# Two halves of a PSUM tile cast first, both remainders after: the key tiles of two head pairs in an attention layer on one Trainium2 core

## The chip, the cores and the metric

The kernel runs on one core of a Trainium2 chip. The metric is the device time of one execution in microseconds (us). The core has engines that run side by side, each with its own list of instructions in a fixed order: TensorE (PE; its weight loads are shown apart as PEld), VectorE (DVE), ScalarE (ACT) and GpSimd (POOL). SyncE (SP) does nothing here but issue transfers. An instruction starts when those ahead of it on its engine have gone and the semaphores that it waits for have been raised.

## The reference

One layer over 1024 positions of width 1024, in float32. The input is normalised and modulated, one projection makes queries, keys, values and gates of 16 heads of width 64, half of the heads attend with a forgetting softmax (FoX), half by stick-breaking, and the gated heads pass an output projection, a residual sum and a second normalisation. Cut to what matters:

```python
u = layer_norm(x) * (1 + scale) + shift
h = u @ w_in                                  # q, k, v, gate of 8 FoX and 8 stick-breaking heads
# FoX head:
s = (q @ k.T) * HEAD_DIM ** -0.5 + (f_q[:, None] - f_k[None, :])
out_fox = softmax(where(causal, s, -inf)) @ v
# stick-breaking head:
z = (q @ k.T) * HEAD_DIM ** -0.5
w = exp(log_sigmoid(z) + sum over later keys of log_sigmoid(-z))   # strictly causal
out_sb = w @ v
y = concat(out_fox * silu(gate_fox), out_sb * silu(gate_sb)) @ w_out
out = layer_norm(alpha * x + gate * y) * ln_g + ln_b
```

## The kernel before

**Numbers in two parts.** TensorE multiplies in the type `fp32r`, which keeps fewer bits than float32. Each operand is therefore held in two parts: a rounded high part (the cast of the value to `fp32r`) and a low part (the value less its high part). A product is the sum of high times high, high times low and low times high, three matmuls into one PSUM tile.

**The work.** The 16 heads go in 8 pairs, index `p` from 0 to 7: pairs 0 to 3 are stick-breaking heads, pairs 4 to 7 FoX heads. In a pair head 0 lies on partitions 0 to 63 and head 1 on partitions 64 to 127. `gen_m(p, m)` projects the queries (`m` = 0), keys (1) and gates (2) of a pair for two chunks `ch` of 512 positions; each chunk is a PSUM tile `m_p_m_ch` of 128 partitions by 512 columns, summed by 24 matmuls (L255 to L257, `m_step`). `gen_v(g)` makes the values of two pairs in 8 tiles of 128 positions (L310 to L312). All these tiles take turns in two PSUM buffers with the tag `acc`: a tile can be begun when the tile before the last has been read by everyone.

**Evacuation of the keys.** When a tile of keys is summed, `evac_k` (L235 to L244) takes it out of PSUM for one head after the other: ScalarE casts the head's 64 partitions into `k` (L240, the high part), SP issues a copy of that part to the other 64 partitions (L242), and VectorE writes the tile less the cast into `kl` (L243, the low part). The program makes every reader of such a PSUM tile wait for the reader written ahead of it, on whatever engine. So in the kernel before the four steps of a tile follow each other in turns: cast of head 0, low part of head 0, cast of head 1, low part of head 1. The buffer is free when the last of them is done.

**Attention.** A unit is (pair, head, block of 128 queries). `att_scores` writes the scores into the PSUM tile `S`, of which there is one buffer (L410, L411). Stick-breaking: ScalarE makes two sigmoids (L430, L431), VectorE one or two scans (L436, L440), GpSimd their product (L444). FoX: VectorE adds the forget rows and finds the row extremes (L417), ScalarE takes the exponential (L423), VectorE the reciprocal (L424), GpSimd scales (L425); on the diagonal block VectorE first adds the mask (L395). ScalarE fetches the next unit's query rows into `qz` (L388). Two units later the weights are transposed by TensorE into a tile `T` (L461), split by ScalarE and VectorE (L463, L464), and multiplied with the values into a tile `pv` (L476), from which the head's output leaves by way of ScalarE, VectorE and GpSimd (L495 to L497).

**The order of the work.** Attention is too uneven to fill TensorE by itself, so the steps of `gen_m` and `gen_v` for later pairs are fillers, set between the attention steps of the pair before. TensorE's order is the order in which the program is written (`manual_schedule`). The order on the other engines and on SP is set by the build's scheduler, which works with durations of its own. Two places matter here. The third pair's keys (`p` = 2) are projected beside the attention of the second pair, and the filler behind them is `gen_v(1)`; its second tile `v_1_1` takes the buffer that the keys' second chunk leaves. The eighth pair's keys (`p` = 7) are projected beside the attention of the seventh, and the filler behind them is `gen_last_g(7)`, the eighth pair's gates, whose two chunks are summed side by side: `m_7_2_0` takes the buffer of the keys' second chunk. Behind every other pair's keys comes the same kind of filler, gates or values, at another point of the attention. Near the eighth pair SP also issues the loads for the output projection: `yr_*` (finished head outputs, L828), `xr_*` (the residual, L863), and `woh_*` and `wol_*` (output weights, L790 and L791).

Of the kernel before, what the change touches and what calls it, by code (L numbers as in the profile page):

```python
# [8 lines left out]
F32 = mybir.dt.float32  # L9
F32R = mybir.dt.float32r  # L10
AF = mybir.ActivationFunctionType
ALU = mybir.AluOpType
# [6 lines left out]
HD = 64  # L19
# [8 lines left out]
def tile_hybrid_layer(  # L28
# [17 lines left out]
    nc = tc.nc  # L46
# [30 lines left out]
    FROW = 12  # L77
    SPACE = 5
    GATE = 3

    def after(*instructions):
        stack = ExitStack()
        for i in instructions:
            stack.enter_context(tc.issue_after(i.ins))
        return stack
# [149 lines left out]
    def evac_k(p, ch, acc, kst, klo, heads):  # L235
        s = slice(ch * 512, ch * 512 + 512)
        for h in heads:
            r = slice(h * HD, h * HD + HD)
            o = slice((1 - h) * HD, (1 - h) * HD + HD)
            first = nc.scalar.copy(kst[h][r, s], acc[r, :])  # L240
            kf = kst[h].bitcast(F32)
            nc.sync.dma_start(kf[o, s], kf[r, s])  # L242
            last = nc.vector.tensor_tensor(klo[r, s], acc[r, :], kf[r, s], op=ALU.subtract)  # L243
        return first, last  # L244

    def evac_g(p, ch, acc, sg):
# [12 lines left out]
    qst, kst, klo, sgt, vt = {}, {}, {}, {}, {}  # L259
# [11 lines left out]
    def evac_m(p, m, ch, acc, heads=(0, 1)):  # L271
        if m == 0:
            evac_q(p, ch, acc, qst[p], heads)
        elif m == 1:
            return evac_k(p, ch, acc, kst[p], klo[p], heads)
        else:
            evac_g(p, ch, acc, sgt[p])
# [364 lines left out]
    for kb in range(NB):  # L642
        last = kb == NB - 1
# [64 lines left out]
    def gen_gate():  # L708
# [4 lines left out]
        nc.gpsimd.tensor_tensor(parts[1], gate, parts[0].bitcast(F32), op=ALU.subtract)  # L713
        for _ in range(GATE):
            yield
# [28 lines left out]
    for kb in range(NB):  # L744
# [13 lines left out]
        if kb < len(evacs):  # L758
            n, h = evacs[kb]
# [209 lines left out]
    for k in range(len(units) + LAG + 1):  # L969
        if k < len(units):  # L970
# [12 lines left out]
            p, h, i = units[k]  # L983
# [86 lines left out]
```

## Time and profile before

| what | value |
| --- | --- |
| median of 3 runs | 689.56 us (689.33 to 689.76) |
| the profiled execution, device time | 689.48 us |
| its span in the trace | 687.8 us |
| granted TensorE clock, mean | 0.997 of full speed |
| TensorE busy | 673.6 us, 98% |
| VectorE busy | 451.8 us, 66% |
| GpSimd busy | 425.8 us, 62% |
| ScalarE busy | 381.9 us, 56% |

A row of the timeline reads: start in us from the span's start, duration in us, engine, line, operation, written tile, read tiles, and the shape. In square brackets stands the idle time of the engine ahead of the row and who ended it. Rows of the view of waits give the waiting engine, tile and line, the one waited for, and us in total, times and longest. An `m` or `S` in a row is a tile name without its numbers, so which pair a row belongs to is read from its place.

### The profile page before, as it was taken

The numbers are of one execution on the slowest core, as the hardware profiler recorded it, in microseconds if no ns is written. First come the engines' busy times: TensorE is split into PE (matmuls) and PEld (weight loads), VectorE is DVE, ScalarE is ACT, GpSimd is POOL, SyncE is SP. The second block draws the span as 40 slices with busy tenths as digits, with TensorE's granted clock in tenths as the row PEclk, the third lists the DMA queues.
The fourth block names the chain that finished last, engine by engine and source line by source line (L and its number), as shares of the span: only waits on it lengthen the run. The fifth ranks groups of instructions, "written<-read, shape, count | busy, mean of one in ns | idle before, by whom it ended". The sixth has DMA issues, their size and how long they took to land.

```text
span 687.8 us, 11790 instructions
## 1 busy us (share of the span) xinstructions
PE 673.6 (98%) x4033; PEld 589.1 (86%) x4033; DVE 451.8 (66%) x924; ACT 381.9 (56%) x862; POOL 425.8 (62%) x555
## 2 busy tenths in 40 slices
PE   7999999999999999999999999999999999999996
PEld 4789898888998888889998888889988889888885
DVE  6895458767656676767675665656565767774645
ACT  4666457856557666666674564655565666531000
POOL 4567978656438565557388887877584364665411
PEclk9999999999999999999999999999999999999998
DMA  8966231011102122112134553444341298143301
GB/s 306 416 235 246 67 110 57 25 41 53 39 9 70 41 55 55 38 47 62 30 133 150 177 170 109 152 152 147 101 135 54 66 296 350 56 157 117 129 31 61
DMA packets 44316, 81.60 MB, mean 119 GB/s; under 512 B 5152, under 2 KB 18784, under 8 KB 43616
## 3 DMA queue, kind: packets, MB, share of 16 engines
q1 hardware_dynamic: 43104, 76.65, 34.1%
q10 hardware_dynamic: 1152, 4.19, 2.1%
q8 instruction: 32, 0.52, 0.3%
q14 instruction: 28, 0.23, 0.1%
HBM read 60.34 MB, written 16.29 MB: 111 GB/s over the span
## 4 chain that ended last, share of the span: by engine, by line
PE 93%; DVE 2%; DMA 1%; POOL 1%; SPq 1%; ACT 1%; issue 0%; POOLq 0%; DVEq 0%
PE m L255 10%; PE pv L476 10%; PE m L256 10%; PE m L257 10%; PE T L461 9%; PE S L411 5%; PE S L410 5%; PE o L853 4%; PE o L851 4%; PE o L852 4%; PE v L310 4%; PE v L311 4%; PE v L312 4%; DMA wss<-in_w_ss_dram 1%; PE st_q L573 1%; PE st_late L569 1%
## 5 line engine op out<-in xcount | busy, mean ns | idle before, releaser
L255 PE MATMUL m<-uh,whi 128*128 128x512 f32 x304 | 126.5, 416 | 0.5 <-DVE kl L243 0.5
L257 PE MATMUL m<-uh,wlo 128*128 128x512 f32 x304 | 119.7, 394 | 0.0
L256 PE MATMUL m<-ul,whi 128*128 128x512 f32 x304 | 119.7, 394 | 0.0
L464 DVE TENSOR_TENSOR pt<-T,pt 128x512 fp32r<-128x512 f32 (+2 forms) x192 | 100.6, 551 | 17.9 <-ACT pt L463 16.8
L444 POOL TENSOR_TENSOR be<-be,kp 128x127 f32<-128x127 f32 (+3 forms) x64 | 77.1, 1206 | 33.7 <-DVE kp L440 24.0
L463 ACT CAST pt<-T 128x512 fp32r<-128x512 f32 (+2 forms) x192 | 85.7, 480 | 16.8 <-PE T L461 13.0
L436 DVE TENSOR_TENSOR_SCAN kp<-kp,floor 128x512 f32<-128x512 f32 (+2 forms) x64 | 65.2, 1018 | 32.1 <-ACT kp L430 31.2
L476 PEld LDWEIGHTS pv<-pt,v 128*128 128x128 f32 (+1 forms) x640 | 77.1, 163 | 4.5 <-DVE pt L464 0.7
L476 PE MATMUL pv<-pt,v 128*128 128x256 f32 (+3 forms) x640 | 80.4, 271 | 0.5 <-DVE pt L464 0.5
L425 POOL TENSOR_SCALAR a<-a,l 128x1024 f32<-128x1024 f32 (+3 forms) x64 | 48.0, 749 | 39.6 <-DVE l L424 26.0
L257 PEld LDWEIGHTS m<-uh,wlo 128*128 128x128 f32 x304 | 57.1, 188 | 13.6
L423 ACT ACTIVATE a<-a,nm 128x1024 f32<-128x1024 f32 (+3 forms) x64 | 49.8, 778 | 34.1 <-DVE nm L417 33.0
L410 PE MATMUL S<-k,q 128*128 128x512 f32 (+5 forms) x192 | 66.5, 348 | 0.2 <-DVE nm L417 0.2
L411 PE MATMUL S<-kl,qz 128*128 128x512 f32 (+5 forms) x192 | 65.5, 342 | 0.0
L255 PEld LDWEIGHTS m<-uh,whi 128*128 128x128 f32 x304 | 57.3, 188 | 9.2 <-DVE kl L243 0.9
L256 PEld LDWEIGHTS m<-ul,whi 128*128 128x128 f32 x304 | 57.4, 189 | 8.0
L497 POOL TENSOR_TENSOR ty<-ty,sg 64x256 f32<-64x256 f32 x64 | 47.4, 741 | 25.0 <-DVE ty L496 12.8
L417 DVE CUSTOM_DVE_ANT_0 a<-S,fb 128x1024 f32<-128x1024 f32 (+3 forms) x64 | 48.3, 755 | 20.5 <-PE S L411 9.8
L430 ACT ACTIVATE kp<-S 128x128 f32<-128x128 f32 (+3 forms) x64 | 41.7, 651 | 31.8 <-PE S L411 29.7
L310 PE MATMUL v<-whi_v,uh 128*128 128x256 f32 (+1 forms) x192 | 56.1, 292 | 0.7 <-DVE kl L243 0.7
L388 ACT CAST qz<-q 64x128 fp32r<-64x128 f32 x128 | 37.4, 295 | 32.9 <-PE S L411 31.8
L311 PE MATMUL v<-whi_v,ul 128*128 128x256 f32 (+1 forms) x192 | 54.2, 282 | 0.0
(291 smaller groups left out, 1609.6 us busy)
## 6 DMA issues: line engine op xcount, KB each, us to landing
raw<-in_w_qkg_dram SPq DMA_DIRECT2D x38, 256.0 KB, 3.0
wss<-in_w_ss_dram SPq DMA_DIRECT2D x5, 1024.0 KB, 9.0
x<-in_x_dram SPq DMA_DIRECT2D x8, 512.0 KB, 7.6
k<-k SPq DMA_DIRECT2D x32, 128.0 KB, 2.4
wg<-in_w_gate_dram SPq DMA_DIRECT2D x8, 512.0 KB, 4.5
raw_o<-in_w_out_dram SPq DMA_DIRECT2D x16, 256.0 KB, 2.7
fb<-f_dr ACTq DMA_DIRECT2D x8, 512.0 KB, 4.2
wo_dr<-whi_o SPq DMA_DIRECT2D x16, 256.0 KB, 2.7
```

Of the source, the lines that this page charges most:

```text
L255: nc.tensor.matmul(acc, hi[:, c], u_hi[kt][:, s], start=(kt == 0), stop=False)
L256: nc.tensor.matmul(acc, hi[:, c], u_lo[kt][:, s], start=False, stop=False)
L257: nc.tensor.matmul(acc, lo[:, c], u_hi[kt][:, s], start=False, stop=(kt == NB - 1))
L310: nc.tensor.matmul(acc[:, :n], u_hi[kt][:, ts_], hi[:, s], start=(kt == 0), stop=False)
L311: nc.tensor.matmul(acc[:, :n], u_lo[kt][:, ts_], hi[:, s], start=False, stop=False)
L410: nc.tensor.matmul(S[:, s, :w], qst[p][h][:, qs], kst[p][h][:, ks], start=True, stop=False)
L411: nc.tensor.matmul(S[:, s, :w], z, klo[p][:, ks], start=False, stop=True)
L436: scan = nc.vector.tensor_tensor_scan(rv, rv, floor[0][:, 512 - n:][:, ::-1], initial=0.0, op0=ALU.mult, op1=ALU.max)
L444: nc.gpsimd.tensor_tensor(be[:, :ke - 1], be[:, :ke - 1], kp[:, 1:ke], op=ALU.mult)
L463: nc.scalar.copy(hi[:, :n, qo:qo + P], t3)
L464: nc.vector.tensor_tensor(lo[:, :n, qo:qo + P], t3, hi.bitcast(F32)[:, :n, qo:qo + P], op=ALU.subtract)
L476: nc.tensor.matmul(acc[:m, q0:256], vt[p][:, kb, h * P:h * P + m], pt[:, kb % 4, q0:], start=start, stop=stop)
```

## The change

For the third and the eighth pair (`p` = 2 and 7) `evac_k` writes both casts first and both low parts behind them. The other six pairs keep their turns. `evac_k` is called for both heads at once for these two pairs, in each of the two chunks; the number of casts, copies and low parts stays as it was.

```diff
+    CASTS_FIRST = (2, 7)
...
             first = nc.scalar.copy(kst[h][r, s], acc[r, :])
             kf = kst[h].bitcast(F32)
             nc.sync.dma_start(kf[o, s], kf[r, s])
-            last = nc.vector.tensor_tensor(klo[r, s], acc[r, :], kf[r, s], op=ALU.subtract)
+            if p not in CASTS_FIRST:
+                last = nc.vector.tensor_tensor(klo[r, s], acc[r, :], kf[r, s], op=ALU.subtract)
+        if p in CASTS_FIRST:
+            for h in heads:
+                r = slice(h * HD, h * HD + HD)
+                last = nc.vector.tensor_tensor(klo[r, s], acc[r, :], kst[h].bitcast(F32)[r, s], op=ALU.subtract)
         return first, last
```

With the waits among the readers of a tile this makes the sequence cast, cast, low part, low part: the first low part waits for the second cast, and the second cast no longer for the first low part. Lines behind the edit have numbers larger by 6 in the changed kernel (L430 is L436), L240 is L241, and the low parts of the two pairs are L249.

Behind the edit the scheduler set some instructions of the other engines in another order; TensorE's order is the same. In the listings below a name such as `k_2_1_1789` is the pair, the head and a running number, and `m_2_1_1` is the tile of the third pair's keys, second chunk.

ScalarE around the third pair's second chunk, in the kernel before:

```order
L463 CAST pt0_1_0_2_1_1931<-T_1_0_4_1_1933 128x128
L240 CAST k_2_0_1788<-m_2_1_1_1868 64x512
L430 ACTIVATE kp_1_0_7_1954<-S_1_0_7_1949 128x1024
L431 ACTIVATE be_1_0_7_1955<-S_1_0_7_1949 128x1024
L388 CAST qz01_81<-q_2_0_1578 64x128
L240 CAST k_2_1_1789<-m_2_1_1_1868 64x512
L463 CAST pt0_1_0_2_0_1922<-T_1_0_5_0_2002 128x4x128
```

and in the changed kernel:

```order
L469 CAST pt0_1_0_2_1_1931<-T_1_0_4_1_1933 128x128
L241 CAST k_2_0_1788<-m_2_1_1_1868 64x512
L241 CAST k_2_1_1789<-m_2_1_1_1868 64x512
L436 ACTIVATE kp_1_0_7_1954<-S_1_0_7_1949 128x1024
L437 ACTIVATE be_1_0_7_1955<-S_1_0_7_1949 128x1024
L394 CAST qz01_81<-q_2_0_1578 64x128
L469 CAST pt0_1_0_2_0_1922<-T_1_0_5_0_2002 128x4x128
```

The second cast moved ahead of the two sigmoids of the unit (1, 0, 7) and of a fetch of query rows. VectorE at the same place, in the kernel before (the two rows of `kp` with `floor` are the two scans):

```order
L464 TENSOR_TENSOR pt1_1_0_2_1_1932<-T_1_0_4_1_1933,pt0_1_0_2_1_1931 128x128
L243 TENSOR_TENSOR kl_2_1790<-m_2_1_1_1868,k_2_0_1788 64x512
L436 SCALAR_TENSOR_TENSOR kp_1_0_7_1954<-kp_1_0_7_1954,floor_889 128x512
L440 SCALAR_TENSOR_TENSOR kp_1_0_7_1954<-kp_1_0_7_1954,floor_889 128x512
L243 TENSOR_TENSOR kl_2_1790<-m_2_1_1_1868,k_2_1_1789 64x512
```

and in the changed kernel:

```order
L470 TENSOR_TENSOR pt1_1_0_2_1_1932<-T_1_0_4_1_1933,pt0_1_0_2_1_1931 128x128
L249 TENSOR_TENSOR kl_2_1790<-m_2_1_1_1868,k_2_0_1788 64x512
L249 TENSOR_TENSOR kl_2_1790<-m_2_1_1_1868,k_2_1_1789 64x512
L442 SCALAR_TENSOR_TENSOR kp_1_0_7_1954<-kp_1_0_7_1954,floor_889 128x512
L446 SCALAR_TENSOR_TENSOR kp_1_0_7_1954<-kp_1_0_7_1954,floor_889 128x512
```

The second low part moved ahead of both scans. In the third pair's first chunk the same two steps move in the same way, ahead of the sigmoids and scans of another unit of the same head; there GpSimd's cast of value weights `whi_v1_3` (L124) also moves ahead of the product `be_1_0_5` (L444). VectorE around the eighth pair's second chunk, in the kernel before:

```order
L417 ISA a_6_1_1_6751,nm_6_1_1_6752<-S_6_1_1_6748,fb_5_6041 128x256
L417 ISA nm_6_1_1_6752 128x1
L243 TENSOR_TENSOR kl_7_6543<-m_7_1_1_6656,k_7_0_6541 64x512
L395 TENSOR_TENSOR fb_5_6041<-fb_5_6041,ps_causal_4153 128x128
L424 RECIPROCAL l_6_1_1_6753<-l_6_1_1_6753 128x1
L417 ISA a_6_1_0_6802,nm_6_1_0_6803<-S_6_1_0_6799,fb_5_6041 128x128
L417 ISA nm_6_1_0_6803 128x1
L243 TENSOR_TENSOR kl_7_6543<-m_7_1_1_6656,k_7_1_6542 64x512
L395 TENSOR_TENSOR fb_6_6439<-fb_6_6439,ps_causal_4153 128x128
```

and in the changed kernel:

```order
L423 ISA a_6_1_1_6751,nm_6_1_1_6752<-S_6_1_1_6748,fb_5_6041 128x256
L423 ISA nm_6_1_1_6752 128x1
L401 TENSOR_TENSOR fb_5_6041<-fb_5_6041,ps_causal_4153 128x128
L249 TENSOR_TENSOR kl_7_6543<-m_7_1_1_6656,k_7_0_6541 64x512
L249 TENSOR_TENSOR kl_7_6543<-m_7_1_1_6656,k_7_1_6542 64x512
L430 RECIPROCAL l_6_1_1_6753<-l_6_1_1_6753 128x1
L423 ISA a_6_1_0_6802,nm_6_1_0_6803<-S_6_1_0_6799,fb_5_6041 128x128
L423 ISA nm_6_1_0_6803 128x1
```

The second low part moved ahead of a reciprocal and of the row step of the unit (6, 1, 0), and the mask step of `fb_5` ahead of both low parts. SP at the eighth pair, in the kernel before:

```order
L242 DMA k_7_0_6541<-k_7_0_6541 64x512
L828 DMA yr_7_4_7205<-y_dr_91 128x3x128
L863 DMA xr_7_7487<-in_x_dram 128x1024
L242 DMA k_7_1_6542<-k_7_1_6542 64x512
L828 DMA yr_4_0_7325<-y_dr_91 128x4x128
L790 DMA woh_0_6822<-wo_dr_92 128x1024
L505 DMA y_dr_91<-ty_6_1_2_6785 64x256
L791 DMA wol_0_6823<-wo_dr_92 128x1024
L790 DMA woh_1_6838<-wo_dr_92 128x1024
```

and in the changed kernel:

```order
L243 DMA k_7_0_6541<-k_7_0_6541 64x512
L243 DMA k_7_1_6542<-k_7_1_6542 64x512
L834 DMA yr_7_4_7205<-y_dr_91 128x3x128
L869 DMA xr_7_7487<-in_x_dram 128x1024
L797 DMA wol_0_6823<-wo_dr_92 128x1024
L796 DMA woh_0_6822<-wo_dr_92 128x1024
L511 DMA y_dr_91<-ty_6_1_2_6785 64x256
L797 DMA wol_1_6839<-wo_dr_92 128x1024
L796 DMA woh_1_6838<-wo_dr_92 128x1024
L834 DMA yr_4_0_7325<-y_dr_91 128x4x128
```

The copy of head 1 moved ahead of two loads, and the load `yr_4_0` behind the first two pairs of output weights.

## The prediction

> **What bounds the kernel now.** I read the page first, then TensorE's waits, then the timeline around the evacuations of the keys.
>
> ```profile
> span 687.8 us, 11790 instructions
> PE 673.6 (98%) x4033; PEld 589.1 (86%) x4033; DVE 451.8 (66%) x924; ACT 381.9 (56%) x862; POOL 425.8 (62%) x555
> PE 93%; DVE 2%; DMA 1%; POOL 1%; SPq 1%; ACT 1%; issue 0%; POOLq 0%; DVEq 0%
> ```
>
> TensorE (PE) is busy 98% of the span and makes 93% of the chain that ended last. Work on any other engine costs nothing until TensorE waits for it, so only TensorE's waits can be worth something. The view of waits, for the weight loads ahead of the matmuls (PEld), has just two that end with line 243, the low parts of the keys; the other two rows stand further on in the time between and are used below:
>
> ```profile
> PEld m L255 <- DVE kl L243: 0.9, 1, 0.9
> PEld v L310 <- DVE kl L243: 0.9, 1, 0.9
> PEld S L410 <- DVE nm L417: 0.6, 1, 0.6
> PEld T L461 <- POOL a L425: 0.5, 1, 0.5
> ```
>
> Columns: us in total, times, longest. Each happens once. The timeline places the one of L310 at 176 us, behind the keys of the third pair, and the one of L255 at 553 us, behind those of the eighth. These are the two pairs that the change touches. No other pair's keys appear in these waits. The third pair, second half of the sequence (its `m` tile with positions 512 to 1023):
>
> ```profile
> 171.05 0.58 ACT L240 CAST k<-m 64x512 fp32r<-64x512 f32 x1 [0.74 <-PE m L257]
> 171.66 0.68 DVE L243 TENSOR_TENSOR kl<-m,k 64x512 fp32r<-64x512 f32 x1 [0.45 <-ACT k L240]
> 171.97 1.03 ACT L430 ACTIVATE kp<-S 128x1024 f32<-128x1024 f32 x1 [0.35 <-PE S L411]
> 172.90 1.02 ACT L431 ACTIVATE be<-S 128x1024 f32<-128x1024 f32 x1
> 173.11 1.22 DVE L436 TENSOR_TENSOR_SCAN kp<-kp,floor 128x512 f32<-128x512 f32 x1 [0.76 <-ACT kp L430]
> 174.11 0.58 ACT L240 CAST k<-m 64x512 fp32r<-64x512 f32 x1
> 174.36 1.28 DVE L440 TENSOR_TENSOR_SCAN kp<-kp,floor 128x512 f32<-128x512 f32 x1
> 175.41 0.27 PE L411 MATMUL S<-kl,qz 128*128 128x128 f32 x1
> 175.67 0.69 DVE L243 TENSOR_TENSOR kl<-m,k 64x512 fp32r<-64x512 f32 x1
> 176.43 0.39 PE L310 MATMUL v<-whi_v,uh 128*128 128x264 f32 x1 [0.74 <-DVE kl L243]
> 176.66 0.28 PE L311 MATMUL v<-whi_v,ul 128*128 128x264 f32 x1
> ```
>
> The reader is to see the detour. The first head's cast is done at 171.63 and its low part at 172.34. The second cast, which waits for that low part, stands on ScalarE behind the two sigmoids and comes at 174.11, and the second low part stands on VectorE behind both scans and ends at 176.36. Then the `acc` buffer is free and TensorE goes on at 176.43. Without a wait the step from the score's product to the second matmul of the values is this (behind a later pair's scores, where nothing is waited for):
>
> ```profile
> 491.15 0.27 PE L411 MATMUL S<-kl,qz 128*128 128x128 f32 x1
> 491.43 0.28 PE L311 MATMUL v<-whi_v,ul 128*128 128x256 f32 x1
> ```
>
> That is 0.28 us against 176.66 - 175.41 = 1.25 us, so **0.97 us** is lost at the third pair (its 264 columns for 256 left aside). The idle time in the row of L310, 0.74 us, is less, as it leaves out the slow step behind the wait. The eighth pair, second half:
>
> ```profile
> 550.14 0.58 ACT L240 CAST k<-m 64x512 fp32r<-64x512 f32 x1 [0.74 <-PE m L257]
> 550.75 0.30 ACT L388 CAST qz<-q 64x128 fp32r<-64x128 f32 x1
> 550.82 0.68 DVE L243 TENSOR_TENSOR kl<-m,k 64x512 fp32r<-64x512 f32 x1
> 551.43 0.27 DVE L395 TENSOR_TENSOR fb<-fb,ps_causal 128x128 f32<-128x128 f32 x1
> 551.70 0.58 ACT L240 CAST k<-m 64x512 fp32r<-64x512 f32 x1
> 552.38 0.39 PE L256 MATMUL m<-ul,whi 128*128 128x512 f32 x1
> 552.61 0.39 PE L257 MATMUL m<-uh,wlo 128*128 128x512 f32 x1
> 552.72 0.69 DVE L243 TENSOR_TENSOR kl<-m,k 64x512 fp32r<-64x512 f32 x1
> 553.45 0.29 DVE L395 TENSOR_TENSOR fb<-fb,ps_causal 128x128 f32<-128x128 f32 x1
> 553.47 0.50 PE L255 MATMUL m<-uh,whi 128*128 128x512 f32 x1 [0.47 <-DVE kl L243]
> 553.80 0.39 PE L256 MATMUL m<-ul,whi 128*128 128x512 f32 x1
> ```
>
> Matmuls of this size start 0.23 us apart (552.38 to 552.61). Undisturbed, L255 would start at 552.84 and the next L256 at 553.07. It starts at 553.80, so **0.73 us** is lost at the eighth pair. Both together are 1.70 us, the most that the change can bring by this route.
>
> **The change part by part.** Nothing is added or removed: same casts, same low parts, same copies of the keys. What goes is the second cast's wait for the first low part; what comes is a wait of the first low part for the second cast.
>
> *Third pair, second half.* The first cast ends at 171.63. How soon the second follows is bounded by the rows of the eighth pair, 0.61 us from start to start (550.14 to 550.75), and by this pair of rows, 0.48 us:
>
> ```profile
> 91.44 0.58 ACT L240 CAST k<-st_k1b 64x512 fp32r<-64x512 f32 x1 [3.46 <-PE st_k1b L573]
> 91.92 0.30 ACT L388 CAST qz<-q 64x128 fp32r<-64x128 f32 x1
> ```
>
> So it ends between 172.11 and 172.24. A low part starts 0.03 us behind its cast (171.63 to 171.66). The second low part follows the first by 0.61 us (550.82 to 551.43, an instruction behind the first head's low part) or 0.73 us (552.72 to 553.45, behind the second head's). It therefore ends between 173.44 and 173.69. TensorE wants the buffer some 0.1 us behind its score product of 175.41, at 175.5, 1.8 us later. The wait is gone whole: **-0.97 us**.
>
> What is late instead: the sigmoids start at 172.2 rather than 171.97, so the score buffer S is free by 174.2 where TensorE first writes it just ahead of 175.41; about 1.1 us remain. The first scan starts at some 173.7 rather than 173.11. This pushes the product on GpSimd behind the second scan by the same 0.6 us, from 175.72 to 176.3 (row below). It runs 1.99 us, and its transposes follow at 183.23, then at 182.3; 4 us remain. Cost: nothing. If that cover were gone, it would cost the 0.2 and 0.6 us by which they are late.
>
> ```profile
> 175.72 1.99 POOL L444 TENSOR_TENSOR be<-be,kp 128x1023 f32<-128x1023 f32 x1 [1.08 <-DVE kp L440]
> 183.23 1.04 PE L461 MATMUL T<-ident,be 128*128 128x128 f32 x8
> ```
>
> *Third pair, first half.* TensorE does not wait for it now. The second cast moves ahead of two sigmoids there too and delays them by at most 0.61 us. The later of them then frees S at 164.97 at the latest, 0.9 us ahead of the next scores:
>
> ```profile
> 163.56 0.80 ACT L431 ACTIVATE be<-S 128x768 f32<-128x768 f32 x1
> 165.88 0.37 PE L410 MATMUL S<-k,q 128*128 128x448 f32 x1
> ```
>
> The scans wait for two low parts, about 1.1 us more; their product has the later transposes as cover, as above. GpSimd takes a cast of value weights ahead of that product. It waits for a TensorE step that this chunk passes before the scan ends, so it falls into time that GpSimd idles. Cost: nothing.
>
> *Eighth pair, second half.* The first cast ends at 550.72, the second between 551.20 and 551.33, and the first low part starts 0.03 us later, at 551.23 to 551.36. The second starts 0.61 to 0.73 us after that and runs 0.69 us: it ends between 552.53 and 552.78. TensorE went on 0.06 us behind that end (553.41 to 553.47), so it can go on at 552.59 to 552.84, and wants to at 552.84. At the early end all 0.73 us comes back. At the late end L255 starts on time but behind a wait, and then the next matmul follows after 0.33 us (553.47 to 553.80) instead of 0.23: 0.63 us. I take the middle, **-0.68 us**.
>
> Here the Trainium skill has a rule. "VectorE: DVE Perf Modes", section "Two Vector instructions with no wait between them", says that an instruction is held until all earlier ones finish when its operands start in another quadrant of 32 partitions than those in front. The trace agrees: behind the first head's low part (partitions 0 to 63) the next starts 0.07 us before its end; behind the second head's (from partition 64) it starts 0.04 us after it. By the rule the two low parts now stand 0.73 us apart, and this place gives 0.63 to 0.73 us; without it, 0.73.
>
> *Eighth pair, first half.* No wait now. One softmax step on ScalarE comes up to 0.61 us later, one reciprocal waits for a second low part; their transposes follow only two score blocks on. Cost: nothing. *Queues.* On SP the second key copy moves forward at each place and the loads of y rows and output weights behind it are reordered; TensorE has no wait on a load in this stretch. ScalarE's own queue issues no load that is passed.
>
> **The sum.** -0.97 - 0.68 = -1.65 us; by the bounds -1.60 to -1.70. The profiled execution took 689.48 us, 1.7 us more than its span, and becomes 687.83 us. The median of the runs is 689.56 us, 0.08 us above; so **687.9 us**, -0.24%.
>
> **The rivals.** A measurement of this kernel tells about 0.2%, 1.38 us, from no change. My forecast is only 0.27 us beyond that.
>
> *Part is taken back further on.* TensorE arrives 0.97 us earlier at everything between 176 and 553 us. Work that runs at the pace of loads does not come earlier with it. For: TensorE already has two short waits there (the two rows of 0.6 and 0.5 us among the waits above), so some cover is at its end. Against: the first of them ends with VectorE's step on TensorE's own scores, so it moves along, and the second ends with GpSimd's scaling of such a step. If half or more of the first gain is lost: 688.4 to 688.9 us.
>
> *Only what the waits show comes back.* 0.74 + 0.47 = 1.21 us (the idle times in the rows of L310 and L255), if the slow step behind a wait is there for another reason: 688.3 us. Against: the 0.28 us of the undisturbed pair.
>
> *The change does not do what it says.* The low part of the first head now waits for the second cast; were another instruction set between them, the end would hardly move, and the time stays at 689.6 us. The order of the changed kernel speaks against it: both stand side by side at all four places.
>
> *Slower.* On SP the load `yr_4_0` now stands behind the first two pairs of output weights, which wait for TensorE. It would go after the second of them, some 0.3 us behind this issue:
>
> ```profile
> 557.85 0.32 SPq L790 DMA_DIRECT2D woh<-wo_dr  x1
> DMA to landing us min/median/max: 2.5/3.7/9.7
> 572.02 0.62 POOL L831 TENSOR_SCALAR whi_y<-yr 128x512 fp32r<-128x512 f32 x1
> ```
>
> With the longest landing it is there at 557.85 + 0.32 + 9.7 = 567.9, or 1.65 less with the gain, 566.2, while GpSimd wants it at 572.02 - 1.65 = 570.4. It begins to delay GpSimd when issue and landing slip by another 4.2 us, and decides when the softmax scaling queued behind it then holds TensorE for over 1.65 us. A slip of 7.5 us would give 687.9 + 3.3 = 691.2 us.
>
> **How the numbers follow.** Forecast 0.57 (687.4 to 688.2 us, from the bounds and 0.2 us of spread); partly taken back 0.22; only the shown waits 0.12; no effect 0.04; slower 0.05. Faster by over 0.2% is the forecast alone, 0.57; within 0.2% are the next three, 0.38; slower 0.05. The range reaches from 687.4 to 689.0 us: it leaves out no effect, slower and a little of the edges.
>
> **What would show it.** In the profile after, no wait of L310 or L255 on a low part; both low parts side by side, the second ending 1.8 us ahead of L310 and within 0.15 us of L255; TensorE's busy time unchanged and its span 1.6 us less. I am wrong if TensorE waits elsewhere between 176 and 553 us for longer than now, if the score products wait for the sigmoids at 165.9 or 175.4 us, or if the low part still ends late at the eighth pair.

## The result, and the profile after

The changed kernel takes 688.16 us, median of 10 runs (687.64 to 689.87), against 689.54 us of the kernel before (10 runs, 689.30 to 691.27). The ratio is 0.9979 with a 95% interval of 0.9970 to 0.9987: 1.4 us faster, by about the 0.2% that the prediction took as what can be told from no change. The forecast was 687.9 us and the range 687.4 to 689.0 us. The profiled execution took 688.05 us, with a span of 686.3 us.

The page of the changed kernel (its span and busy times), and three rows of its view of waits for the weight loads:

```profile
span 686.3 us, 11792 instructions
...
PE 672.7 (98%) x4033; PEld 588.6 (86%) x4033; DVE 451.7 (66%) x924; ACT 381.7 (56%) x862; POOL 425.7 (62%) x555
```

```profile
PEld S L416 <- DVE nm L423: 0.6, 1, 0.6
...
PEld T L467 <- POOL a L431: 0.3, 1, 0.3
PEld m L261 <- DVE kl L249: 0.2, 1, 0.2
```

The wait of the values (now L316) on a low part is gone, and that of the gates (now L261) fell from 0.9 to 0.2 us. The wait for GpSimd's scaling (L431) in the second row is new: it stands at 438 us and is taken up below. It is not the one that the kernel before had in such a row (0.5 us, at 515 us). That one is still there, with the same 0.46 us, but the view now names another instruction. The timeline of the changed kernel at the third pair's second half:

```profile
171.10 1.19 ACT L241 CAST k<-m 64x512 fp32r<-64x512 f32 x2 [0.74 <-PE m L263]
...
172.31 1.03 ACT L436 ACTIVATE kp<-S 128x1024 f32<-128x1024 f32 x1
172.31 1.41 DVE L249 TENSOR_TENSOR kl<-m,k 64x512 fp32r<-64x512 f32 x2 [1.06 <-ACT k L241]
...
173.75 1.22 DVE L442 TENSOR_TENSOR_SCAN kp<-kp,floor 128x512 f32<-128x512 f32 x1
...
175.46 0.27 PE L417 MATMUL S<-kl,qz 128*128 128x128 f32 x1
175.56 0.34 PE L316 MATMUL v<-whi_v,uh 128*128 128x264 f32 x1
175.74 0.28 PE L317 MATMUL v<-whi_v,ul 128*128 128x264 f32 x1
...
176.37 2.00 POOL L450 TENSOR_TENSOR be<-be,kp 128x1023 f32<-128x1023 f32 x1 [1.69 <-DVE kp L446]
...
182.31 1.04 PE L467 MATMUL T<-ident,be 128*128 128x128 f32 x8
```

Both casts stand together, then both low parts, which end at 172.31 + 1.41 = 173.72 us, 1.84 us ahead of L316. From the score's product to the second matmul of the values TensorE needs 175.74 - 175.46 = 0.28 us; before it was 1.25. That is 0.97 us. The product on GpSimd starts 0.65 us later than before, at 176.37, and the transposes that read it come at 182.31 without a wait.

The same at the eighth pair's second half:

```profile
549.29 1.19 ACT L241 CAST k<-m 64x512 fp32r<-64x512 f32 x2 [0.74 <-PE m L263]
...
550.52 1.39 DVE L249 TENSOR_TENSOR kl<-m,k 64x512 fp32r<-64x512 f32 x2
...
551.53 0.39 PE L262 MATMUL m<-ul,whi 128*128 128x512 f32 x1
...
551.76 0.39 PE L263 MATMUL m<-uh,wlo 128*128 128x512 f32 x1
...
551.96 0.19 PEld L261 LDWEIGHTS m<-uh,whi 128*128 128x128 f32 x1 [0.24 <-DVE kl L249]
551.99 0.48 PE L261 MATMUL m<-uh,whi 128*128 128x512 f32 x1
...
552.30 0.39 PE L262 MATMUL m<-ul,whi 128*128 128x512 f32 x1
```

The low parts end at 550.52 + 1.39 = 551.91 us, 2.62 us behind the start of the first cast, and the weight load goes 0.05 us later. L261 starts on time, 0.23 us behind L263, but behind a wait, and L262 follows after 0.31 us. From L263 to the second L262 it is 552.30 - 551.76 = 0.54 us; before it was 553.80 - 552.61 = 1.19. That is 0.65 us.

These two times, called the intervals of the two places below, from the score's product to the second matmul of the values (the third place, 1.25 us before) and from the last matmul of one chunk to the second of the other (the eighth place, 1.19 us before), are the measure in all that follows. They don't depend on where TensorE stood before.

Between the two places a little is given back. Ahead of the first place the changed kernel is 0.05 us late (175.41 before, 175.46 after), behind it 0.92 us early (176.66 and 175.74), at the second place 0.85 us (552.61 and 551.76), behind it 1.50 us (553.80 and 552.30). Most of the 0.07 us between goes in one place, shown here for the kernel before:

```profile
437.39 1.02 POOL L425 TENSOR_SCALAR a<-a,l 128x896 f32<-128x896 f32 x1
...
439.20 0.93 PEld L461 LDWEIGHTS T<-ident,a 128*128 128x128 f32 x7
439.43 0.93 PE L461 MATMUL T<-ident,a 128*128 128x128 f32 x7
440.12 0.48 PE L410 MATMUL S<-k,q 128*128 128x512 f32 x1
```

and for the changed kernel:

```profile
434.65 1.30 POOL L126 TENSOR_TENSOR wlo_o<-raw_o,whi_o 128x512 fp32r<-128x512 f32 x1 [1.02 <-DMA wo_dr<-wlo_o]
...
437.45 1.01 POOL L431 TENSOR_SCALAR a<-a,l 128x896 f32<-128x896 f32 x1
...
438.51 0.75 PEld L467 LDWEIGHTS T<-ident,a 128*128 128x128 f32 x7 [0.28 <-POOL a L431]
...
438.52 0.98 PE L467 MATMUL T<-ident,a 128*128 128x128 f32 x7
439.26 0.48 PE L416 MATMUL S<-k,q 128*128 128x512 f32 x1
```

In this execution GpSimd had waited 1.02 us for a transfer of the output weights, and scales the softmax at the same time as before (437.39 and 437.45). TensorE comes 0.91 us earlier and meets it. Before, the weight load of the transposes went 0.79 us behind the end of the scaling (438.41 to 439.20); now it goes 0.05 us behind it (438.46 to 438.51), after 0.28 us without work. The step from the transposes to the next scores grows from 0.69 to 0.74 us, so 0.05 us is lost. How much cover GpSimd leaves here changes from run to run: with the third pair alone changed (first experiment) it did not wait for the transfer, scaled at 436.73, and the load again went 0.81 us behind its end.

### The profile page after: what moved, and what is told of

It reads as the page before. It is cut to its first block, busy times and chain, and to the rows that moved or that the text cites. A ratio compares the mean times of both kernels' runs of the same rounds, so it can differ in the third digit from the quotient of the medians.

```text
span 686.3 us, 11792 instructions
## 1 busy us (share of the span) xinstructions
PE 672.7 (98%) x4033; PEld 588.6 (86%) x4033; DVE 451.7 (66%) x924; ACT 381.7 (56%) x862; POOL 425.7 (62%) x555
## 4 chain that ended last, share of the span: by engine, by line
PE 88%; DMA 4%; POOL 3%; DVE 2%; issue 1%; SPq 1%; ACT 0%; POOLq 0%
PE pv L482 10%; PE m L261 9%; PE m L262 9%; PE m L263 9%; PE T L467 9%; PE S L417 4%; PE S L416 4%; PE o L859 4%; PE o L857 4%; PE o L858 4%; PE v L316 4%; PE v L317 4%; PE v L318 4%; DMA wss<-in_w_ss_dram 3%; DMA raw<-in_w_qkg_dram 2%
## 5 line engine op out<-in xcount | busy, mean ns | idle before, releaser
L261 PE MATMUL m<-uh,whi 128*128 128x512 f32 x304 | 126.4, 416 | 0.0
L262 PE MATMUL m<-ul,whi 128*128 128x512 f32 x304 | 119.7, 394 | 0.0
L263 PE MATMUL m<-uh,wlo 128*128 128x512 f32 x304 | 119.7, 394 | 0.0
L431 POOL TENSOR_SCALAR a<-a,l 128x1024 f32<-128x1024 f32 (+3 forms) x64 | 48.0, 750 | 40.0 <-DVE l L430 26.4
L263 PEld LDWEIGHTS m<-uh,wlo 128*128 128x128 f32 x304 | 57.1, 188 | 13.6
L261 PEld LDWEIGHTS m<-uh,whi 128*128 128x128 f32 x304 | 57.3, 188 | 8.5 <-DVE kl L249 0.2
L262 PEld LDWEIGHTS m<-ul,whi 128*128 128x128 f32 x304 | 57.4, 189 | 8.0
L436 ACT ACTIVATE kp<-S 128x128 f32<-128x128 f32 (+3 forms) x64 | 41.7, 651 | 31.6 <-PE S L417 29.5
L316 PE MATMUL v<-whi_v,uh 128*128 128x256 f32 (+1 forms) x192 | 56.0, 292 | 0.0
```

The source lines that it names most:

```text
L261: nc.tensor.matmul(acc, hi[:, c], u_hi[kt][:, s], start=(kt == 0), stop=False)
L262: nc.tensor.matmul(acc, hi[:, c], u_lo[kt][:, s], start=False, stop=False)
L263: nc.tensor.matmul(acc, lo[:, c], u_hi[kt][:, s], start=False, stop=(kt == NB - 1))
L316: nc.tensor.matmul(acc[:, :n], u_hi[kt][:, ts_], hi[:, s], start=(kt == 0), stop=False)
```

## The experiments

Theory: at each of the two places TensorE waited for the last low part because steps of the evacuation stood in the queues behind sigmoids, scans and row steps; the gain is the sum of the two, whatever the other pairs do. Rivals: the turns themselves (the second cast's wait for the first low part) were what cost; or any shorter evacuation is worth something; or TensorE follows VectorE's end one for one.

**One place at a time.**

```diff
-    CASTS_FIRST = (2, 7)
+    CASTS_FIRST = (2,)
```

> Casts first for the third pair alone. Theory (two separate waits, each worth its own detour): TensorE moves ahead by 0.97 us at the third pair's second chunk and by nothing at the eighth, and gives back 0.05 us where GpSimd's scaling comes late at 438 us, as in the changed kernel; -0.9 us against before, some 688.6 us. The wait of the eighth pair's gates on a low part stays at 0.47 us. Rival (the two places hang together, or the order set elsewhere brings the gain): the eighth place moves too, and the time is that of the changed kernel, 688.1 us.

```diff
-    CASTS_FIRST = (2, 7)
+    CASTS_FIRST = (7,)
```

> Casts first for the eighth pair alone. Theory: no shift up to 553 us, the wait of 0.74 us behind the third pair's keys stays, TensorE moves ahead by 0.66 us at the gates of the eighth pair; the wait for GpSimd at 438 us is not there, since TensorE arrives there no earlier than before. -0.66 us, some 688.9 us. Rival (part of the second gain was paid by the earlier arrival): the eighth place brings 0.73 us or under 0.5 us.

The third pair alone takes 688.61 us against 689.55 us of the kernel before (ratio 0.9986, 95% interval 0.9977 to 0.9995; so in all brackets below), the eighth alone 689.01 us (0.9991, 0.9983 to 1.0000, which by the time alone is hardly told from no change). The first of the rows that follow is from the run with the third pair alone:

```profile
552.84 0.50 PE L261 MATMUL m<-uh,whi 128*128 128x512 f32 x1 [0.47 <-DVE kl L245]
```

and this from the run with the eighth alone:

```profile
176.88 0.39 PE L316 MATMUL v<-whi_v,uh 128*128 128x264 f32 x1 [0.74 <-DVE kl L245]
```

Each run keeps the other wait to the hundredth. The interval at the third place is 0.29 us in the first and 1.24 in the second, that at the eighth 1.19 and 0.54. The two add: 0.96 + 0.65 = 1.61 us by the trace. GpSimd's scaling at 438 us held nothing in either profile. With the third pair alone it had moved forward with TensorE, as said above, so that the 0.05 us expected there is a miss, and the loss in the changed kernel's profile goes with the wait for a transfer in that one execution.

**All pairs.**

```diff
-    CASTS_FIRST = (2, 7)
+    CASTS_FIRST = tuple(range(8))
```

> Casts first for all eight pairs. Theory: only the two places where TensorE waits for a low part count, so the other six pairs bring nothing: 687.9 to 688.3 us as the changed kernel, and TensorE shifts by steps at 176 and 553 us only. Rival (a shorter evacuation is worth something behind every pair's keys): six more pairs at some 0.1 us and more give 687.5 us or less. Second rival: a cast that moves ahead of sigmoids or exponentials holds TensorE at a place with less cover, a new wait of up to 0.6 us, 688.7 us.

692.06 us, 2.5 us slower than before (1.0035, 1.0023 to 1.0048). All theories had it wrong: at the two places the gain is there (0.29 and 0.53 us), but the fourth to the seventh pair lose more. The second rival named the kind for one of them. The dearest is the seventh pair, shown in the kernel before:

```profile
458.22 0.68 DVE L243 TENSOR_TENSOR kl<-m,k 64x512 fp32r<-64x512 f32 x1 [2.27 <-ACT k L240]
458.82 0.54 DVE L464 TENSOR_TENSOR pt<-T,pt 128x384 fp32r<-128x384 f32 x1
...
459.29 1.21 DVE L417 CUSTOM_DVE_ANT_0 a<-S,fb 128x1024 f32<-128x1024 f32 x1
...
460.53 0.69 DVE L243 TENSOR_TENSOR kl<-m,k 64x512 fp32r<-64x512 f32 x1
```

and in the run with all pairs:

```profile
460.18 1.39 DVE L249 TENSOR_TENSOR kl<-m,k 64x512 fp32r<-64x512 f32 x2 [2.88 <-ACT k L241]
...
461.60 1.23 DVE L423 CUSTOM_DVE_ANT_0 a<-S,fb 128x1024 f32<-128x1024 f32 x1
...
462.75 0.55 DVE L470 TENSOR_TENSOR pt<-T,pt 128x384 fp32r<-128x384 f32 x1
...
463.36 0.75 PE L482 MATMUL pv<-pt,v 128*64 128x256 f32 x5 [1.46 <-DVE pt L470]
```

With turns the low half of the attention weights (L464) went between the two low parts. Now it stands behind both and behind a row step of 1.2 us, and the product with the values waits 1.46 us for it. Its view of waits has four such waits, 4.1 us together, and one of the scores for a sigmoid, 0.7 us:

```profile
PEld pv L482 <- DVE pt L470: 4.1, 4, 1.6
...
PEld S L416 <- ACT be L437: 0.7, 1, 0.7
```

In the kernel before the first of these is there once, with 0.7 us, and the second not at all. New are therefore 3.4 + 0.7 = 4.1 us of waits, against 0.96 + 0.66 = 1.62 us gained at the two places: 2.5 us more, as measured.

**Turns kept, queued work moved.** The steps of the two pairs' evacuation wait for each other as before, but the sigmoids, exponentials and query fetches of the next unit stand behind the second cast on ScalarE, and by that the scans behind the second low part on VectorE. `after` sets an order on one engine and adds no wait.

```diff
+        if p in TURNS_AHEAD:
+            held[:] = [first, last]
         return first, last
...
+            with after(*held):
+                nc.scalar.activation(v3(kp), S[:, :ns, :w], AF.Sigmoid, scale=-1.0)
...
+                with after(*held):
+                    att_query(units[k + 1])
```

> The turns stay (cast, low part, cast, low part, each waiting for the one ahead), but for the third and eighth pair the sigmoids, exponentials and query fetches of the next unit are queued behind the second cast on ScalarE, and the scans behind the second low part on VectorE. Theory (the loss lies in work queued between the steps, not in the turns): at the third pair the second low part ends 2.6 us behind the start of the first cast, at 173.7 us, well ahead of 175.5, and the whole 0.97 us comes; at the eighth it ends at 552.83 us, 0.05 us too late, and 0.58 us comes; together -1.5 us, 688.0 to 688.3 us. Rival (the dropped wait itself brings the gain): the time stays at 689.5 us. Second rival: the two sigmoids come 0.9 us later and hold the scores at 175.4 us, 688.8 us.

688.95 us against 689.55 (0.9987, 0.9979 to 0.9996), above the 688.0 to 688.3 us expected. The third place is as in the changed kernel, 0.29 us. At the eighth a wait came up that none of the theories had:

```profile
552.04 0.33 PE L415 MATMUL S<-kl,qz 128*128 128x128 f32 x1 [0.97 <-ACT qz L392]
```

The query fetch, held back too, now holds the scores for 0.97 us. In the next run the fetch is free, and VectorE's next row step is held behind the last low part:

```diff
-                with after(*held):
-                    att_query(units[k + 1])
+                att_query(units[k + 1])
...
+            with after(*held_rows):
+                rows = nc.vector.tensor_tensor_reduce(out=v3(a), in0=S[:, :ns, :w], in1=v3(f),
```

> As the run with the turns kept, but the query fetches are free again and only the sigmoids and exponentials are queued behind the second cast, the scans and the next row step behind the second low part. Theory (the loss lies in the queued work, not in the turns): the third place brings 0.94 to 0.97 us; at the eighth the evacuation takes 2.70 us from the first cast's start, as in the run before this, TensorE wants it after 2.64 us, and 0.57 to 0.63 us comes; no wait for a query fetch. Together -1.55 us, 688.0 to 688.2 us, as the changed kernel. Rival (turns cost time of their own): 0.3 us or more less than the changed kernel brings, 688.4 us or more.

688.08 us against 689.64 (0.9977, 0.9968 to 0.9986), the time of the changed kernel. The first and the last step of the evacuation at the third pair in this run:

```profile
171.16 0.58 ACT L242 CAST k<-m 64x512 fp32r<-64x512 f32 x1 [0.75 <-PE m L261]
...
173.11 0.69 DVE L245 TENSOR_TENSOR kl<-m,k 64x512 fp32r<-64x512 f32 x1 [0.65 <-ACT k L242]
```

and at the eighth:

```profile
549.29 0.58 ACT L242 CAST k<-m 64x512 fp32r<-64x512 f32 x1 [0.74 <-PE m L261]
...
549.98 0.68 DVE L245 TENSOR_TENSOR kl<-m,k 64x512 fp32r<-64x512 f32 x1
550.58 0.27 DVE L399 TENSOR_TENSOR fb<-fb,ps_causal 128x128 f32<-128x128 f32 x1
550.69 0.58 ACT L242 CAST k<-m 64x512 fp32r<-64x512 f32 x1 [0.49 <-DVE kl L245]
...
551.31 0.69 DVE L245 TENSOR_TENSOR kl<-m,k 64x512 fp32r<-64x512 f32 x1 [0.46 <-ACT k L242]
```

In turns, but with nothing of note between them, the four steps take 2.64 us at the third pair (171.16 to 173.80; 5.31 in the kernel before) and 2.71 us at the eighth (549.29 to 552.00), against 2.62 us at both with the casts first. The intervals are 0.29 and 0.63 us. So the turns cost 0.09 us at the eighth place and nothing at the third; the rest of the two detours was the work queued between the steps. The rival falls. A run that drops the wait and leaves the queues as they were was not made.

**How much cover there is.** The first head's low part of the second chunk is written again, once for both pairs or three times more for the third; scans and reciprocals stay behind it.

```diff
+    EXTRA = {2: 1, 7: 1}
...
+                for _ in range(1 + (EXTRA.get(p, 0) if ch == 1 and h == 0 else 0)):
                     last = nc.vector.tensor_tensor(klo[r, s], acc[r, :], kst[h].bitcast(F32)[r, s], op=ALU.subtract)
```

> The changed kernel, with the first head's low part of the third and eighth pair's second chunk written twice (the same values), so that VectorE has one such instruction more ahead of the last. Theory (1.8 us of cover at the third place, none at the eighth): nothing at 176 us, where the last low part now ends at 174.4 us; at the eighth TensorE goes on 0.6 to 0.7 us later than in the changed kernel. 688.7 to 688.9 us. By the rule of the Trainium skill on two Vector instructions without a wait between them, the repeat (same partitions) starts 0.61 us behind the first and the other head's 0.70 us behind the repeat. Rival (TensorE follows VectorE's end at both places): 0.65 us later at each, 689.4 us.

688.74 us against 689.64 (0.9987, 0.9978 to 0.9996). Both places in this run, VectorE's group at the third and at the eighth, and TensorE behind the latter:

```profile
172.27 2.12 DVE L252 TENSOR_TENSOR kl<-m,k 64x512 fp32r<-64x512 f32 x3 [1.06 <-ACT k L243]
...
550.41 2.11 DVE L252 TENSOR_TENSOR kl<-m,k 64x512 fp32r<-64x512 f32 x3
...
552.57 0.50 PE L265 MATMUL m<-uh,whi 128*128 128x512 f32 x1 [0.53 <-DVE kl L252]
```

The third place stays at 0.29 us, the eighth goes from 0.54 to 1.26, so 0.72 us later (0.6 to 0.7 expected). TensorE follows VectorE's end only where there is no cover. For the rule of the Trainium skill ("VectorE: DVE Perf Modes", section "Two Vector instructions with no wait between them") this run was no test: the repeat writes what the low part ahead wrote, so the program makes it wait for that one. Some (2.12 - 0.69) / 2 = 0.72 us lie between two starts, on average; the 0.61 us expected for the repeat is a miss.

```diff
-    EXTRA = {2: 1, 7: 1}
+    EXTRA = {2: 3}
```

> The changed kernel, with the first head's low part of the third pair's second chunk written four times instead of once. Theory: the last low part ends at 175.6 to 175.8 us and TensorE wants the buffer at 175.5 us, so the cover of 1.8 us is used up: a wait of 0.1 to 0.3 us and 0.1 us for the slow step behind it; the third place brings 0.5 to 0.8 us instead of 0.97, and the scans, 2 us later, cost nothing since their product is wanted at 182.3 us only. 688.3 to 688.6 us. Rival (the cover is shorter than 1.8 us, or the late scans hold the transposes): the third place brings nothing or the transposes at 182 us wait, 689.2 us or more.

688.52 us against 689.64 (0.9981, 0.9972 to 0.9990). The third place here:

```profile
172.74 3.56 DVE L252 TENSOR_TENSOR kl<-m,k 64x512 fp32r<-64x512 f32 x5 [1.06 <-ACT k L243]
...
176.35 0.39 PE L320 MATMUL v<-whi_v,uh 128*128 128x264 f32 x1 [0.20 <-DVE kl L252]
```

3.56 - 1.41 = 2.15 us more on VectorE, and the interval grows from 0.28 to 0.70 us. The cover was 2.15 - 0.42 = 1.7 us, close to the 1.84 us read from the rows; the 0.42 us still holds the slow step behind the wait, some 0.1 us, so the real cover is that much larger. The scans, later by as much, held nothing up.

**One cast for both heads.** For the two pairs one cast takes all 128 partitions into head 1's tile, one low part follows, and three copies instead of two bring the rows into place.

```diff
+            first = nc.scalar.copy(kst[1][:, s], acc)
+            nc.sync.dma_start(k0[:HD, s], k1[:HD, s])
+            nc.sync.dma_start(k0[HD:, s], k1[:HD, s])
+            last = nc.vector.tensor_tensor(klo[:, s], acc, k1[:, s], op=ALU.subtract)
+            nc.sync.dma_start(k1[:HD, s], k1[HD:, s])
```

> For the third and eighth pair one cast takes the tile of both heads (128 partitions) into the tile of head 1, one low part follows for both, and three copies instead of two bring the heads' rows into place. Theory: a row of 128 partitions takes as long as one of 64, so the evacuation takes 1.3 us instead of 2.6; the third place brings 0.97 us as before, the eighth the whole 0.73 us, with no wait of the gates on a low part. 688.0 us. Rival (the copies become the bound): the scores of the eighth pair's first unit, 4.6 us behind the copy's issue, now wait for a second copy, 0.5 us and more, 688.6 us.

688.18 us against 689.64 (0.9983, 0.9974 to 0.9991). The eighth place:

```profile
549.69 0.59 ACT L240 CAST k<-m 128x512 fp32r<-128x512 f32 x1 [0.74 <-PE m L266]
...
550.37 0.69 DVE L243 TENSOR_TENSOR kl<-m,k 128x512 fp32r<-128x512 f32 x1
...
553.94 0.47 SPq L244 DMA_DIRECT2D k<-k  x1
```

The evacuation is over at 551.06, 1.37 us behind the cast's start, and the interval is 0.46 us: the whole 0.73 us is back, with no wait for a low part and none for the copies, though the third copy, which waits for the first two, is issued at 553.94 only. By the trace this is 0.08 us better than the change; the time doesn't show it, since 0.08 us is far less than its spread.

**The order of the low parts on VectorE.** Each low part of the two pairs is cut into two halves of columns, in two orders, with no wait between the four.

```diff
-            for h in heads:
+            for h, c in ((0, 0), (0, 1), (1, 0), (1, 1)):
                 r = slice(h * HD, h * HD + HD)
-                last = nc.vector.tensor_tensor(klo[r, s], acc[r, :], kst[h].bitcast(F32)[r, s], op=ALU.subtract)
+                a = slice(c * 256, c * 256 + 256)
+                sa = slice(ch * 512 + c * 256, ch * 512 + c * 256 + 256)
+                last = nc.vector.tensor_tensor(klo[r, sa], acc[r, a], kst[h].bitcast(F32)[r, sa], op=ALU.subtract)
```

> The changed kernel with each low part of the third and eighth pair cut into two column halves (64 x 256), in the order head 0, head 0, head 1, head 1, with no wait between the four. A row of this size takes 0.42 us here. By the rule of the Trainium skill on two Vector instructions without a wait between them, a half that follows one of the same head starts 0.07 us before its end, one that follows the other head's is held: 0.35 + 0.43 + 0.35 + 0.42 = 1.55 us for the four, 0.16 us more than the 1.39 us of the two whole ones; TensorE goes on 0.1 to 0.2 us later at the eighth pair than in the changed kernel and no later at the third. Rival (no such rule: each follows the end of the one ahead): 1.71 us for the four, as in the run with the halves in turns, and 0.3 us later.

```diff
-            for h, c in ((0, 0), (0, 1), (1, 0), (1, 1)):
+            for h, c in ((0, 0), (1, 0), (0, 1), (1, 1)):
```

> The same four halves in the order head 0, head 1, head 0, head 1. By the rule every one is held: 0.43 x 3 + 0.42 = 1.71 us, 0.32 us more than the two whole ones, and TensorE goes on 0.3 us later at the eighth pair than in the changed kernel; at the third nothing. Rival (no such rule, all overlap by 0.07 us): 1.47 us, as the run with the halves by head. The two runs differ in nothing but the order.

The four halves at the eighth pair, by head:

```profile
550.72 1.53 DVE L251 TENSOR_TENSOR kl<-m,k 64x256 fp32r<-64x256 f32 x4
```

and with the heads in turns:

```profile
550.71 1.73 DVE L251 TENSOR_TENSOR kl<-m,k 64x256 fp32r<-64x256 f32 x4
```

1.53 and 1.73 us, where 1.55 and 1.71 were expected. The same four instructions take 0.20 us longer when each has other partitions than the one ahead. This is what the Trainium skill states in the section named above, of instructions without a wait, and both rivals fall. TensorE goes on 0.19 and 0.40 us later than in the changed kernel (intervals of 0.73 and 0.94 us for 0.54); the second is 0.1 us more than expected. In both, TensorE's weight load goes 0.11 us behind the end of the last low part, against 0.05 us in the changed kernel; no row shows why. The times, 688.44 and 688.51 us against 689.68 (0.9983, 0.9973 to 0.9992, and 0.9982, 0.9972 to 0.9991), don't tell the two apart.

## Why the prediction was right

*What bounds the kernel, and where.* Right. The two waits on line 243 were the places, and the runs with one pair each gave them back one by one.

*Third pair, -0.97 us.* Right: 1.25 to 0.28 us. That the slow step behind the wait belongs to the loss, and not only the idle time of 0.74 us, decided this number; the rival that counted idle times alone (1.21 us for both) falls with 0.97 + 0.65.

*What is late instead.* Right in kind and size: the scan starts at 173.75 (some 173.7 forecast), the product at 176.37 (176.3), the transposes at 182.31 (182.3), and the scores at 175.39 wait for nothing.

*Eighth pair, -0.68 us.* It brought 0.65 us. The sign "no wait of L255 on a low part" did not come true: 0.24 us of the load's wait are left, as at the late end of the forecast, where 0.63 us come. The second cast starts 0.61 us behind the first and the second low part 0.70 behind the first one, held as the rule has it, so the low parts end 2.62 us behind the first cast's start; the forecast had 2.39 to 2.64 and took the middle. The bound from the row of this very place, 0.61 us, was the one to take.

*What goes.* Here the prediction was off. It described the detour through the queues, but as what goes it named only the second cast's wait for the first low part, and this wait was not what cost: the run with the turns kept puts it at 0.09 us at the eighth place and at nothing at the third. What had to go was the place in the two queues behind sigmoids, scans and row steps, which the change moved as well. That the scheduler does so because the two casts can now go together is likely, but not shown. The number held because it was worked out from the changed order, in which both are in.

*The sum, -1.65 us.* It was 1.62 us at the two places. The profiled execution went from 689.48 to 688.05 us, -1.43; the difference is the 0.05 us by which it was late ahead of the first place, the 0.07 us between the places, and some 0.07 us behind the second that I can't place. The medians differ by 1.38 us, and the median of 688.16 us is 0.1 us above its own profiled execution.

*Partly taken back.* The rival's price (half the first gain) was far too high: 0.05 us in this profile. What the prediction held against it came true for the two waits that it named, which moved along with TensorE by 0.86 us at the same length: 532.92 to 532.06 us (0.64 us, for VectorE's row step) and 515.30 to 514.44 us (0.46 us). For the second the reason given was wrong, though the view before names it: this wait can't be for GpSimd's scaling, since in the changed kernel the scaling begins at 514.40 and ends at 515.09, when the weight load has long gone. VectorE's low half of the weights, which stands ahead of it in both profiles, is likelier; it is not shown. And the prediction overlooked the scaling at 438 us, which did not move along in this execution. Strictly, its sign of being wrong (TensorE waits elsewhere between 176 and 553 us for longer than now) came true there, by 0.28 us of the weight load's time.

*Slower.* The load `yr_4_0` was no cost. GpSimd's cast `whi_y` moved along with TensorE, from 572.02 to 570.52 us.

*TensorE's busy time* was to stay; it is 672.7 us for 673.6. The groups of the later stages agree to 0.1 us; most of the difference lies in the first stage's products with the identity (7.6 us for 7.9 and 3.4 for 3.8).

## What to carry to other kernels

When a buffer comes free late, list what stands on each engine between the steps that empty it: here a chain of 2.6 us had become 5.3 us in the queues at the third pair, and putting its steps side by side brought all of the 0.97 us there and 0.56 to 0.65 of the 0.73 us at the eighth, in turns or not. Do it where the trace shows someone waiting for the buffer, and read first what the moved steps are set ahead of: the same edit for all pairs made the kernel 2.5 us slower. After a gain look for the next engine that doesn't move along; here it was GpSimd at 438 us, in a profile in which a transfer had held it by 1.02 us.

## What the hardware showed that was not expected

A cast and a low part over 128 partitions take what they take over 64 (0.59 and 0.69 us, for 0.58 and 0.68 to 0.69). Four VectorE instructions of 0.42 us took 1.53 or 1.73 us by their order alone. And executions differ in the first stage: the score product ahead of the first place stood at 175.41 us in the kernel before and at 175.86 in the run with the eighth pair alone, at 175.46 in the changed kernel and at 175.73 in the run with the third alone, though the edit changes nothing up to there between the first two or between the last two. At the first scores, near 91 us, the two differences were already there. This spread of 0.3 to 0.5 us covers effects of 0.1 us in the time, not in an interval.
